# Where three pieces of ScalarE, VectorE and TensorE work stand in the attention projections of a hybrid attention and mLSTM kernel

## The chip, the core and the metric

The kernel runs on one core of one Trainium2 chip. The metric is the device time of one execution in microseconds. Three runs of the kernel before took 1403.57, 1403.64 and 1404.39 us; the median is 1403.64 us.

## What is computed

The model is two layers deep on 512 tokens of width 1024: a dilated window attention, a gated FFN, an mLSTM mixer and a second gated FFN, each with its norm and residual. The change touches only the projections of the attention, and the work that is woven into them:

```python
proj = (xn @ w_in).reshape(B, S, N_GROUPS, 3, ATTN_HEADS, ATTN_HEAD_DIM)   # 3 groups, q k v, 8 heads of 128
for g, (window, dilation) in enumerate(((128, 1), (512, 4), (2048, 16))):
    q = apply_partial_rope(proj[:, :, g, 0], positions) * scale            # only the first 32 of 128 rows turn
    k = apply_partial_rope(proj[:, :, g, 1], positions)
    o, lse = dilated_window_attention(q, k, proj[:, :, g, 2], window, dilation)
wts = softmax(stack(lses), axis=0)                                          # over the three groups
out = (sum over g of wts[g] * o[g]).reshape(B, S, 1024) @ w_out
```

## The kernel before

Every float32 product is made of three matmuls: each operand is split into a rounded part ("hi", written by a cast on ScalarE, L224) and the rest ("lo", a subtraction on VectorE, L226), and hi·hi, lo·hi and hi·lo are added in PSUM. In the trace ACT is ScalarE, DVE VectorE, PE TensorE, SP and POOL the engines that issue DMAs.

The eight heads go in four pairs, a0 to a3. From pair 1 on, group 0 of a pair is projected plainly, and groups 1 and 2 (names a1g1, a1g2 and so on) as a "unit" each, `qk_unit`: the two 1024x256 weight blocks (q and k) and the tokens are cut in halves, and seven products of a Strassen kind give what eight would. Their order is P1, P5, P6, P2, P7, P3, P4; each is 24 matmuls of 128x128 by 128x256. They share three PSUM banks: P1 and P2 add up in `c`, P5 and P3 in `p`, P6, P7 and P4 in `u`. Behind each product stands `finish`: after P1 ScalarE copies bank c to bank u (L903); after P5 and P6 it copies banks p and u to SBUF (`vu`, L906 and L908); after P2 and P4 ScalarE packs the 32 rows to be rotated (`rot`, L897) and copies the bank to the q tile (L916); after P7 and P3 VectorE adds the bank to `vu` into the k tile (L923), and ScalarE packs again. The bank p that P5 of unit g2 fills is the one that the L916 copy behind P4 of unit g1 empties, so the first matmul of P5 waits for that copy (the row `a1g2p <- a1g_q` of the PE waits).

The weights of a unit come in four pieces W11, W12, W21, W22 by SP's DMA queue (L863) into a ring of raw buffers (`a1g2W` and so on); a piece's load is issued when the buffer's last reader is done, which is mostly an L226. `prepare_part` forms differences of pieces on VectorE (`less`, L871) and then the split (L224, L226). `Feed` prepares the splits ahead of their product: `pop` hands over one and fills up to `ahead` (3 here).

Work of other kinds is put into this stream by a clock of ticks (`defer(n, fn)` runs fn n ticks on, `advance` is a tick; a unit ticks after its products 2, 4, 6 and 7). Two kinds matter. First, `rope` turns the packed rows on VectorE (L605 to L614) and returns `back`, which copies them back into q and k on ScalarE: L620 for group 0 (four instructions for q, four for k), L622 for the others. Second, the attention of the pair before, whose places are the table `RUN_AT` (scores of groups 1 and 2, the joint softmax, L792/L795 weights, L801 transposes to and from DRAM, and `values`, L819/L824) and the scores of group 0 of the current pair, `scores0` (matmuls L698, VectorE's mask and maximum L704, exponentials L741 on ScalarE), placed by `SCORES0_AT`. What shares an engine goes in written order, helped by `behind`, which issues work behind the instruction last written on a named engine.

Of the kernel before, what the change touches and what calls it, by code (L numbers as in the profile page):

```python
# [32 lines left out]
C1 = 6.28125  # L33
C2 = float(np.float32(np.uint32(np.float32(TWO_PI - C1).view(np.uint32) & 0xFFFFF000).view(np.float32)))
C3 = float(np.float32(TWO_PI - C1 - C2))
SCORES0_AT = (None, 6, 6, 5)
RUN_AT = (1, (4, 5, 8, 8, 9), (11, 12), (2, 3, 1))
RUN3_AT = (1, (4, 5, 7, 7, 8), (11, 12), (2, 3, 1))
LAST_AT = (1, (2,), (), (1, 1, 1))
STACK_AT = (9, 11, 15, 17)  # L40
HEAD_AT = ((9, 10, 12), (10, 11, 13), (12, 13, 15), (13, 14, 16), (15, 16, 18), (16, 17, 19), (18, 19, 21),
# [33 lines left out]
def tile_hybrid_dilated_attn_mlstm(  # L75
# [205 lines left out]
    class Feed:  # L281
# [6 lines left out]

        def pop(self, _=0):
            whl = self.ready.pop(0) if self.ready else self.plan.pop(0)()  # L290
            while self.plan and len(self.ready) < self.ahead:
                self.ready.append(self.plan.pop(0)())
            return whl

    ends = {}

# [105 lines left out]
    with ExitStack() as actx:  # L402
# [485 lines left out]
        def qk_unit(pr, g, qk):  # L888
            nm = "a%dg%d" % (pr, g)
            last = pr == HEADS // 2 - 1 and g == 2  # L890
            target = {"P1": "c11", "P2": "c11", "P5": "p5", "P3": "p5", "P6": "u", "P7": "u", "P4": "u"}
            two_m = lambda t: t.rearrange("p (m s) -> p m s", m=2)
            acc = {}
            rot = vu = None

            def pack(q, src):
                nc.scalar.activation(two_m(rot[0][quarter(q)]), src, AF.Copy)  # L897

            def finish(name):
                nonlocal rot, vu  # L900
                if name == "P1":
                    acc["u"] = acc_tile(nm + "u")
                    nc.scalar.activation(acc["u"], acc["c11"], AF.Copy)  # L903
                elif name == "P5":
                    vu = ap.tile([P, 2, SEQ], F32, tag="vu", name=nm + "vu")
                    nc.scalar.activation(vu[:, 0], acc["p5"], AF.Copy)  # L906
                elif name == "P6":
                    nc.scalar.activation(vu[:, 1], acc["u"], AF.Copy)  # L908
                elif name in ("P2", "P4"):
                    th = int(name == "P4")  # L910
                    src = two_m(acc[target[name]])
                    if th == 0:
                        t = ap.tile([P, 2, SEQ], F32, tag="rot", name="rot")
                        rot = t[:, 0], t[:, 1]
                    pack(th, src[:R])
                    nc.scalar.activation(halves(qk[0], th), src, AF.Copy)  # L916
                    if last and th:
                        rope(qk, rot, False, 1, 2, True)
                else:
                    th = int(name == "P7")  # L920
                    out = halves(qk[1], th)
                    with behind_scores():
                        nc.vector.tensor_tensor(out, two_m(acc[target[name]]), two_m(vu[:, 1 - th]), op=ALU.add)  # L923
                    pack(2 + th, out[:R])
                    if last and th == 0:
                        rope(qk, rot, False, 0, 1, True)
                        rope(qk, rot, False, 2, 4, True)

            for n, name in enumerate(QK_ORDER):
                key = target[name]  # L930
                if name in ("P1", "P5"):
                    acc[key] = acc_tile(nm + key)
                whl = feed.pop()
                with fenced():
                    for m in range(2):
                        for k in range(4):
                            for a, b in SPLITS:
                                if name in ("P1", "P2", "P4"):
                                    x_ = pair[b][k + 4 * (name != "P1")][:, HALF * (name == "P4"):HALF * (1 + (name == "P4"))]
                                else:  # L940
                                    x_ = sum_part(name, b, k)
                                nc.tensor.matmul(acc[key][:, m * HALF:(m + 1) * HALF], whl[a][:, k, m * P:(m + 1) * P], x_,
                                                 start=(name in ("P1", "P5") and m == 0 and k == 0 and (a, b) == SPLITS[0]),
                                                 stop=(m == 1 and k == 3 and (a, b) == SPLITS[-1]), skip_group_check=True)
                finish(name)
                if n == 6 and not last:
                    back = rope(qk, rot, False)
                    if g == 2:
                        back()
                    else:  # L950
                        defer(1, back)
                if n in (1, 3, 5, 6):
                    advance()

        def project_pair(pr, qks, then=None):
            nm = "a%d" % pr
            for g in range(3):
                base = g * 3 * D + pr * 256
                qk = []
                qks.append(qk)  # L960

                box = []
                if pr and g:
                    qk.extend(tok_tile("%sg%d_%s" % (nm, g, "qk"[part])) for part in range(2))
                    qk_unit(pr, g, qk)
                    continue

                def rot(box=box):
                    if not box:
                        if pr:  # L970
                            box.extend(npl.tile([P, SEQ], F32, tag=tag, name="rot") for tag in ("rbc", "ssum"))
                        else:
                            t = ap.tile([P, 2, SEQ], F32, tag="rot", name="rot")
                            box.extend((t[:, 0], t[:, 1]))
                    return box
                for part in range(2):
                    t = tok_tile("%sg%d_%s" % (nm, g, "qk"[part]))

                    def evac(m, acc, t=t, rot=rot, g=g, part=part):
                        to = rot()  # L980
                        views = (in_order, by_block) if g == 0 else (lambda x: x,) * 2
                        if pr == 0:
                            nc.vector.tensor_tensor(views[0](t[:, m]), views[1](acc), views[1](rbc), op=ALU.mult)
                        else:
                            nc.vector.tensor_copy(views[0](t[:, m]), views[1](acc))
                        for th in range(2):
                            q = 2 * part + th
                            nc.scalar.activation(packed(to, q, m, g == 0), turned((t, t), q, m, g == 0), AF.Copy)
                    if pr == 0 and g == 0 and part == 0:
                        def first_evac(evac=evac):  # L990
                            bc_hook()
                            for m in range(2):
                                evac(m, facc[m])
                        defer(1, first_evac)
                    else:
                        if pr == 0 and g == 2 and part == 1:
                            defer(1, lambda: renew(range(4)))
                        project(pair, w_in, base + part * D, KC, evac, "%sg%d%s" % (nm, g, "qk"[part]), ready=feed,
                                amid=pr > 0 and part == 1)
                    qk.append(t)  # L1000
                    if part == 1:
                        turn = lambda qk=qk, rot=rot, g=g: rope(qk, rot(), g == 0)
                        if pr == 0 and g == 2:
                            postponed.append(lambda: turn()())
                        else:
                            defer(3 if pr else 1, turn())
                    if pr == 0 and 1 <= g:
                        step = 2 * (g - 1) + part
                        (lambda: sum_of("S3"), lambda: sum_of("S4"), lambda: None, lambda: None)[step]()
                        for key in ((), ("W12", "W22"), (), ())[step]:  # L1010
                            for hf in range(2):
                                behind(load_block, 0, key, hf, engine=mybir.EngineType.SP)
                if g == 0 and then is not None:
                    then()
                if g == 0 and pr == 0:
                    first_values()
# [231 lines left out]
        for pr in range(1, HEADS // 2):  # L1248
            qks = []
            following = attention_pair(pr, qks)  # L1250
            follow(todo, RUN3_AT if pr == 3 else RUN_AT)
            project_pair(pr, qks, lambda fn=following[0], pr=pr: defer(SCORES0_AT[pr], lambda: run(fn)))
            todo = following
        last_values, last_bring = todo[3], todo[6]
        run(lambda: todo[1]((1,)))
# [1111 lines left out]
```

## Time and profile before

| | us |
|---|---|
| median of three runs | 1403.64 |
| the profiled execution, its own time | 1403.1 |
| its span in the trace | 1401.2 |
| PE busy | 1373.2 (98 %) |
| DVE busy | 1110.8 (79 %) |
| ACT busy | 798.4 (57 %) |

The granted TensorE clock is 0.997 on the mean. The projections of the pairs 1 to 3 lie between about 200 and 430 us of the span. Rows of the timeline give the start, the duration, engine, line and operation, the output and input, and in square brackets the idle time of the engine just before, with what ended it. In the list of waits a row names the engine and what it wanted to do, what it waited for, then the total, the number of times and the longest, in us. In a table of windows the columns are the busy time of PE, PE's weight loads, DVE, ACT and POOL, the granted clock (PEclk, 1.00 is full), the busy share of the DMA engines and GB/s.

### The profile page before, as it was taken

Reading aid. Unit: us, or ns where it says so; the run is one execution under the profiler, and the core shown is the slowest. Engines: PE = TensorE matmul, PEld = TensorE weight load, DVE = VectorE, ACT = ScalarE, POOL = GpSimd, SP = SyncE. Lnnn points to the kernel's source line nnn. Section 1 sums busy time; section 2 is a strip of 40 time slices with the busy share of each in tenths; the row PEclk is TensorE's granted clock in tenths of the full one; section 3 lists DMA queues with packets and bytes.
Section 4 is the critical chain, followed back from the end, with each engine's and each line's share of the span. In section 5 each row is a group of like instructions: output and inputs, shape, how many; then the busy total and the mean of one; then the engine's idle time right before and its main releaser. Section 6 shows DMA issues by size and latency. Waiting matters only on the chain. (4 is left out here: it accounts for less than half of the span.)

```text
span 1401.2 us, 22635 instructions
## 1 busy us (share of the span) xinstructions
PE 1373.2 (98%) x8740; PEld 1245.5 (89%) x8740; DVE 1110.8 (79%) x1853; ACT 798.4 (57%) x1334; POOL 163.3 (12%) x240
## 2 busy tenths in 40 slices
PE   9999999999979999999999999999999999999997
PEld 7888889889878888999999998888888899999886
DVE  7758669596877289877877898898858987888887
ACT  6556566666655155444566464786534544458854
POOL 3000011111011001000000100113201240001213
PEclk9999999999999999999999999999999999999999
DMA  8534246547375447333253643334334563335963
GB/s 286 183 120 136 89 138 194 160 121 233 89 235 155 150 133 164 121 121 108 90 169 87 144 143 88 93 79 106 95 117 117 136 191 121 121 108 132 196 164 99
DMA packets 140068, 193.82 MB, mean 138 GB/s; under 512 B 8980, under 2 KB 104788, under 8 KB 139960
## 3 DMA queue, kind: packets, MB, share of 16 engines
q1 hardware_dynamic: 119552, 139.81, 31.8%
q0 software_dynamic: 18752, 51.43, 16.0%
q8 instruction: 69, 1.13, 0.3%
q10 hardware_dynamic: 1656, 1.12, 0.2%
q14 instruction: 39, 0.32, 0.1%
HBM read 167.30 MB, written 22.54 MB: 135 GB/s over the span
## 5 line engine op out<-in xcount | busy, mean ns | idle before, releaser
L1670 POOL DMA_DIRECT2D f1T<-in_ffn_w_out_dram x15 | 17.8, 1185 | 209.0 <-DMA f1P_2w_w<-in_ffn_w_out_dram 136.2
L1645 POOL DMA_DIRECT2D f0S<-in_ffn_w_out_dram x10 | 8.7, 874 | 261.0 <-DVE f0hid L1562 173.0
L2202 POOL DMA_DIRECT2D hD<-hB x32 | 21.7, 698 | 68.3 <-DVE hB L2199 68.3
L256 PE MATMUL mo<-n_h,mo_k_l 128*128 128x512 f32 x64 | 25.3, 395 | 0.0
L256 PE MATMUL mo<-n_h,mo_k_h 128*128 128x512 f32 x64 | 25.2, 394 | 0.0
L256 PE MATMUL mo<-n_l,mo_k_h 128*128 128x512 f32 x64 | 25.2, 393 | 0.0
L256 PE MATMUL awo<-ao_h,awo_k_h 128*128 128x512 f32 x64 | 25.2, 393 | 0.0
L256 PE MATMUL mwo<-yo_l,mwo_k_h 128*128 128x512 f32 x64 | 25.1, 392 | 0.0
L256 PE MATMUL mqk<-n_h,mqk_k_h 128*128 128x512 f32 x64 | 25.1, 392 | 0.0
L256 PE MATMUL mqk<-n_l,mqk_k_h 128*128 128x512 f32 x64 | 25.1, 392 | 0.0
L256 PE MATMUL awo<-ao_l,awo_k_h 128*128 128x512 f32 x64 | 25.1, 392 | 0.0
L256 PE MATMUL f0j<-n_h,f0j_h 128*128 128x512 f32 x64 | 25.0, 391 | 0.0
L256 PE MATMUL f1j<-n_h,f1j_h 128*128 128x512 f32 x64 | 25.0, 391 | 0.0
L256 PE MATMUL mwo<-yo_h,mwo_k_l 128*128 128x512 f32 x64 | 25.0, 391 | 0.0
L256 PE MATMUL mqk<-n_h,mqk_k_l 128*128 128x512 f32 x64 | 25.0, 391 | 0.0
L256 PE MATMUL awo<-ao_h,awo_k_l 128*128 128x512 f32 x64 | 25.0, 390 | 0.0
L256 PE MATMUL f1j<-n_h,f1j_l 128*128 128x512 f32 x64 | 24.9, 390 | 0.0
L256 PE MATMUL f0j<-n_h,f0j_l 128*128 128x512 f32 x64 | 24.9, 390 | 0.0
L256 PE MATMUL f0j<-n_l,f0j_h 128*128 128x512 f32 x64 | 24.9, 389 | 0.0
L256 PE MATMUL f1j<-n_l,f1j_h 128*128 128x512 f32 x64 | 24.9, 389 | 0.0
L256 PE MATMUL mwo<-yo_h,mwo_k_h 128*128 128x512 f32 x64 | 24.8, 391 | 0.0
L226 DVE TENSOR_TENSOR v1P_l<-v1W,v1P_h 128x1024 fp32r<-128x1024 f32 x14 | 17.1, 1223 | 9.3 <-ACT v1P_h L224 9.3
(2617 smaller groups left out, 5890.0 us busy)
## 6 DMA issues: line engine op xcount, KB each, us to landing
f0j_w<-in_ffn_w_in_dram SPq DMA_DIRECT2D x17, 512.0 KB, 5.0
f1j_w<-in_ffn_w_in_dram SPq DMA_DIRECT2D x17, 512.0 KB, 6.0
f1T<-in_ffn_w_out_dram POOLq DMA_DIRECT2D x15, 512.0 KB, 7.1
f0hid<-in_ffn_w_in_dram SPq DMA_DIRECT2D x9, 512.0 KB, 6.1
f1hid<-in_ffn_w_in_dram SPq DMA_DIRECT2D x9, 512.0 KB, 5.0
v0W<-in_attn_w_in_dram SPq DMA_DIRECT2D x8, 512.0 KB, 6.4
v1W<-in_attn_w_in_dram SPq DMA_DIRECT2D x8, 512.0 KB, 4.4
awo_k_w<-in_attn_w_out_dram SPq DMA_DIRECT2D x8, 512.0 KB, 4.7
```

What stands on the lines that cost most here:

```text
L226: nc.vector.tensor_tensor(lo[:, :n], raw[:, :n], hi[:, :n].bitcast(F32), op=ALU.subtract)
L256: nc.tensor.matmul(acc, whl[a][:, k, m * P:(m + 1) * P], pairs[b][kk], start=(kk == 0 and (a, b) == SPLITS[0]), stop=(kk == nk - 1 and (a, ...
L1645: nc.gpsimd.dma_start(t, src[1][:, ks], accum_op=ALU.add)
L1670: nc.gpsimd.dma_start(view(to), weight_rows(hk * UNITS + u, n), accum_op=ALU.add)
L2202: nc.gpsimd.dma_start(hD[k // 4].rearrange("(b i) x -> i b x", i=R)[:, :, c0:c0 + R], t[R * a_:R * (a_ + 1)])
```

## The change

Three edits, all in the stream of the pairs 1 to 3.

- The scores of group 0 of pair 3 are asked for 6 ticks on instead of 5, as those of the pairs 1 and 2, and pair 3's table of places for the attention of pair 2 (`RUN3_AT`) is replaced by that of the others.
- `qk_unit` calls `feed.fill(ahead + 1)` right behind `finish`, so the next split is written there, ahead of the deferred work of the tick, and no longer at the next `pop`.
- The `back` of a rope is written behind the instruction that is last on ScalarE at that time (`behind(..., engine=ACT)`).

```diff
-SCORES0_AT = (None, 6, 6, 5)
+SCORES0_AT = 6
 RUN_AT = (1, (4, 5, 8, 8, 9), (11, 12), (2, 3, 1))
-RUN3_AT = (1, (4, 5, 7, 7, 8), (11, 12), (2, 3, 1))
...
         def pop(self, _=0):
             whl = self.ready.pop(0) if self.ready else self.plan.pop(0)()
-            while self.plan and len(self.ready) < self.ahead:
+            self.fill(self.ahead)
+            return whl
+
+        def fill(self, n):
+            while self.plan and len(self.ready) < n:
                 self.ready.append(self.plan.pop(0)())
-            return whl
...
                 finish(name)
+                feed.fill(feed.ahead + 1)
                 if n == 6 and not last:
                     back = rope(qk, rot, False)
                     if g == 2:
                         back()
                     else:
-                        defer(1, back)
+                        defer(1, lambda: behind(back, engine=ACT))
...
-                            defer(3 if pr else 1, turn())
+                            back = turn()
+                            defer(3 if pr else 1, lambda back=back: behind(back, engine=ACT))
...
-            follow(todo, RUN3_AT if pr == 3 else RUN_AT)
-            project_pair(pr, qks, lambda fn=following[0], pr=pr: defer(SCORES0_AT[pr], lambda: run(fn)))
+            follow(todo, RUN_AT)
+            project_pair(pr, qks, lambda fn=following[0]: defer(SCORES0_AT, lambda: run(fn)))
```

Lines after the change have other numbers: L224 and L226 become L223 and L225, L620 L622, L801 L803, L871 L873, L897 L899, L906 and L908 become L908 and L910, L916 L918, L698 L700, L704 L706.

The first place is ScalarE in unit g1 of pair 1. Before, the back of group 0 stands around the copies of P5 and P6 of that unit (L906, L908):

```order
L224 ACTIVATE a1g1P_h<-a1g1W_1585 128x1024
L906 ACTIVATE a1g1vu<-a1g1p_1847 128x512
L620 ACTIVATE a1g_q<-rot 32x4x64 x4
L224 ACTIVATE a1g1P_h<-a1g1W_1587 128x1024
L908 ACTIVATE a1g1vu<-a1g1u 128x512
L620 ACTIVATE a1g_k<-rot 32x4x64 x4
```

After, the same eight copies (now L622) stand at the end of the unit, behind the last cast, which is that of P6 of unit g2, and ahead of the packing (L899) and the bank copy (L918) of P4 of unit g1:

```order
L899 ACTIVATE rot<-a1g_k 32x512 x2
L223 ACTIVATE a1g2P_h<-a1g2W_1853 128x1024
L622 ACTIVATE a1g_q<-rot 32x4x64 x4
L622 ACTIVATE a1g_k<-rot 32x4x64 x4
L899 ACTIVATE rot<-a1g1u 32x512
L918 ACTIVATE a1g_q<-a1g1u 128x2x256
```

The pairs 2 and 3 have the same pattern. The second place is VectorE at the same time of pair 1. Before, the transposes of pair 0 (L801) stand ahead of the lo of P3 (from W_1585) and of P4:

```order
L614 TENSOR_TENSOR rot<-rot 128x512
L226 TENSOR_TENSOR a1g1P_l<-a1g1W_1583,a1g1P_h 128x1024
L801 STREAM_TRANSPOSE a0pB<-a0p_1529 128x15x4x32
L226 TENSOR_TENSOR a1g1P_l<-a1g1W_1585,a1g1P_h 128x1024
L226 TENSOR_TENSOR a1g1P_l<-a1g1W_1587,a1g1P_h 128x1024
```

After, the lo of P3 stands ahead of the transposes:

```order
L616 TENSOR_TENSOR rot<-rot 128x512
L225 TENSOR_TENSOR a1g1P_l<-a1g1W_1583,a1g1P_h 128x1024
L225 TENSOR_TENSOR a1g1P_l<-a1g1W_1585,a1g1P_h 128x1024
L803 STREAM_TRANSPOSE a0pB<-a0p_1529 128x15x4x32
L225 TENSOR_TENSOR a1g1P_l<-a1g1W_1587,a1g1P_h 128x1024
```

The third place is unit g2 of pair 3, the last of the phase. On VectorE before, the lo of P3 (from W_3525) stands behind the rotation of q's first rows (L605, L606) and all sixteen rows of the scores' mask and maximum (L704):

```order
L226 TENSOR_TENSOR a3g2P_l<-a3g2W_3486,a3g2P_h 128x1024
L605 STREAM_SHUFFLE rot<-rot 32x512
L606 TENSOR_TENSOR rot<-rot,cosn 32x512
L704 ISA a3p_3778,a3own<-a3s_3780,acst 128x128
...
L704 ISA a3p_3779,a3own<-a3s_3795,acst 128x256
L704 ISA a3own 128x1
L736 TENSOR_SCALAR a3nb<-a3own 128x4
L226 TENSOR_TENSOR a3g2P_l<-a3g2W_3525,a3g2P_h 128x1024
```

After, the lo of P3 (from W_3518), the lo of P4 and the lo of the first value weights (`a3g12v`) stand ahead of them:

```order
L225 TENSOR_TENSOR a3g2P_l<-a3g2W_3485,a3g2P_h 128x1024
L616 TENSOR_TENSOR rot<-rot 128x512
L873 TENSOR_TENSOR a3g2W_3556<-a3g2W_3556,a3g2W_3483 128x1024
L225 TENSOR_TENSOR a3g2P_l<-a3g2W_3518,a3g2P_h 128x1024
L225 TENSOR_TENSOR a3g2P_l<-a3g2W_3556,a3g2P_h 128x1024
L225 TENSOR_TENSOR a3g12v_k_l<-a3g12v_k_w,a3g12v_k_h 128x1024
L607 STREAM_SHUFFLE rot<-rot 32x512
L608 TENSOR_TENSOR rot<-rot,cosn 32x512
L609 TENSOR_TENSOR rot<-rot,sinn 32x512
L613 TENSOR_TENSOR a3g_q<-rot 32x2x256
L706 ISA a3p_3845,a3own<-a3s_3847,acst 128x128
```

On TensorE the matmuls of `scores0` of pair 3 stood between P5 and P6 of unit g2; after, they stand between P2 and P7, as in the pairs 1 and 2. Nothing else on TensorE changes place.

## The prediction

> **What bounds the kernel now.** I read the shares first, then the waits of the engine with the largest share, then the timeline around the waits that the change can touch.
>
> ```profile
> span 1401.2 us, 22635 instructions
> PE 1373.2 (98%) x8740; PEld 1245.5 (89%) x8740; DVE 1110.8 (79%) x1853; ACT 798.4 (57%) x1334; POOL 163.3 (12%) x240
> ```
>
> TensorE is busy for 98 % of the span, and the change adds or removes no matmul. It can only move time between TensorE's waits. So the question is which waits of TensorE the three edits remove and which they make. The list of its waits, longest first, with the rows of the pairs 1 to 3:
>
> ```profile
> PE a3g2p L942 <- DVE a3g2P_l L226: 5.5, 1, 5.5
> PE a3g2p L942 <- ACT a3g_q L916: 2.0, 1, 2.0
> PE a3o L819 <- DMA a3pT<-a3pD: 1.6, 1, 1.6
> ...
> PE a2g1u L942 <- ACT a2g1vu L908: 1.1, 1, 1.1
> PE a1g2p L942 <- ACT a1g_q L916: 1.0, 1, 1.0
> ...
> PE a2g2p L942 <- ACT a2g_q L916: 0.7, 1, 0.7
> ```
>
> Two kinds matter. One is a single stall of 5.5 us, P3 of unit g2 of pair 3 waiting for its lo. The other is the wait at the seam of the two units of each pair: P5 of g2 needs bank p, and ScalarE's L916 copy behind P4 of g1 is late by 1.0, 0.7 and 2.0 us. The change removes the first and puts 2.9 us of ScalarE work ahead of the second.
>
> **The change part by part.** The seam of pair 1 first, on ScalarE and VectorE:
>
> ```profile
> 214.43 1.46 ACT L620 ACTIVATE a1g_q<-rot 32x256 f32<-32x256 f32 x4 [1.50 <-DVE rot L614]
> 217.49 1.45 ACT L620 ACTIVATE a1g_k<-rot 32x256 f32<-32x256 f32 x4
> ...
> 224.95 0.68 DVE L923 TENSOR_TENSOR a1g_k<-a1g1p,a1g1vu 128x512 f32<-128x512 f32 x1
> 226.60 1.23 DVE L871 TENSOR_TENSOR a1g2W<-a1g2W,a1g2W 128x1024 f32<-128x1024 f32 x1 [0.97 <-DMA a1g2W<-in_attn_w_in_dram]
> ...
> 227.94 1.06 ACT L224 ACTIVATE a1g2P_h<-a1g2W 128x1024 fp32r<-128x1024 f32 x1 [1.65 <-DVE a1g2W L871]
> 229.03 0.59 ACT L897 ACTIVATE rot<-a1g1u 32x512 f32<-32x512 f32 x1
> 229.64 0.60 ACT L916 ACTIVATE a1g_q<-a1g1u 128x512 f32<-128x512 f32 x1
> ...
> 230.29 0.50 PE L942 MATMUL a1g2p<-S,a1g2P_h 128*128 128x256 f32 x2 [1.01 <-ACT a1g_q L916]
> ```
>
> ScalarE has no gap between the cast of P6 of g2 (227.94) and the end of the bank copy (230.24): 2.30 us for cast, pack and copy. In the new order the two backs, 1.46 + 1.45 = 2.91 us, stand between cast and pack. So from the start of that cast the copy now ends 2.30 + 2.91 = 5.21 us later. If nothing else moved, P5 would start 2.91 us late in each pair. But the cast itself waits (1.65 us) for a difference on VectorE, which waits for a DMA (0.97 us): piece W22 of g2's weights. That load is issued when a buffer comes free, which is the end of the lo of g1's P3, here behind the transposes:
>
> ```profile
> 215.46 2.17 DVE L801 STREAM_TRANSPOSE a0pB<-a0p 128x1920 f32<-128x1920 f32 x1
> 217.55 2.31 DVE L226 TENSOR_TENSOR a1g1P_l<-a1g1W,a1g1P_h 128x1024 fp32r<-128x1024 f32 x2
> ...
> 218.76 1.50 SPq L863 DMA_DIRECT2D a1g2W<-in_attn_w_in_dram  x2
> ```
>
> Now that lo stands ahead of the transposes. It can start at 215.5, since its cast is done at 212.4, so the load is issued about 2.1 us earlier and should land near 224.5 instead of 226.6. Then the difference is bound by VectorE itself: its k addition (224.95) waits for P3 on TensorE, which comes 0.35 us earlier, because ScalarE's copy of P6 (L908) no longer stands behind the back and TensorE's wait for it (0.4 us) goes. So the difference starts near 225.3 in place of 226.60, the cast 1.3 us earlier at 226.6, and the copy ends at 226.6 + 5.21 = 231.8 against 230.24. **Pair 1: +1.6 us.** Its bounds: +1.3 (all of the 1.65 us idle time goes) to +2.9 (the load lands no earlier).
>
> The same in pair 2:
>
> ```profile
> 299.84 1.23 DVE L226 TENSOR_TENSOR a2g2P_l<-a2g2W,a2g2P_h 128x1024 fp32r<-128x1024 f32 x1 [0.32 <-ACT a2g2P_h L224]
> ...
> 306.09 1.23 DVE L871 TENSOR_TENSOR a2g2W<-a2g2W,a2g2W 128x1024 f32<-128x1024 f32 x1 [0.42 <-DMA a2g2W<-in_attn_w_in_dram]
> ...
> 307.43 1.07 ACT L224 ACTIVATE a2g2P_h<-a2g2W 128x1024 fp32r<-128x1024 f32 x1 [1.10 <-DVE a2g2W L871]
> ```
>
> Less can be won back here: the DMA wait is 0.42 us, and a VectorE wait for a cast of 0.32 us goes because that cast no longer stands behind a back. Cast at 307.43 − 0.74 = 306.7, copy done 5.21 later at 311.9, against P5's start at 309.78. **Pair 2: +2.2 us** (bounds +1.8, all 1.10 us back, to +2.9).
>
> In pair 3 the seam was already worse, and for another reason:
>
> ```profile
> 384.08 1.13 DVE L795 TENSOR_SCALAR a2p<-a2p,a2cf 128x256 f32<-128x256 f32 x4
> 385.13 1.22 DVE L871 TENSOR_TENSOR a3g2W<-a3g2W,a3g2W 128x1024 f32<-128x1024 f32 x1
> ...
> 386.29 2.00 ACT L224 ACTIVATE a3g2P_h<-a3g2W 128x1024 fp32r<-128x1024 f32 x2 [1.46 <-DMA a3g2W<-in_attn_w_in_dram]
> 388.93 0.60 ACT L916 ACTIVATE a3g_q<-a3g1u 128x512 f32<-128x512 f32 x1
> 389.58 0.50 PE L942 MATMUL a3g2p<-S,a3g2P_h 128*128 128x256 f32 x2 [1.96 <-ACT a3g_q L916]
> ```
>
> Pair 3's own table puts four weight multiplications (1.13 us) ahead of the difference, and two casts stand ahead of the copy. With the common table the difference comes first, at about 383.8, and one cast of the two goes behind the copy: cast 385.05, copy done at 390.26. **Seam of pair 3: +0.7 us** (bounds −0.3, when the cast starts a microsecond earlier still, to +2.0, the 2.9 less the one cast).
>
> Then the large stall. VectorE's queue in unit g2 of pair 3:
>
> ```profile
> 403.36 1.06 ACT L224 ACTIVATE a3g12v_k_h<-a3g12v_k_w 128x1024 fp32r<-128x1024 f32 x1 [3.28 <-DMA a3g12v_k_w<-in_attn_w_in_dram]
> ...
> 404.94 0.01 DVE L605 LOAD_MASK_SELECT rot<-rot  x1 [8.42 <-ACT rot L897]
> ...
> 406.29 0.27 DVE L704 CUSTOM_DVE_ANT_0 a3p<-a3s,acst 128x128 f32<-128x128 f32 x1
> ...
> 408.85 1.21 DVE L226 TENSOR_TENSOR a3g2P_l<-a3g2W,a3g2P_h 128x1024 fp32r<-128x1024 f32 x1
> ...
> 410.11 0.58 PE L942 MATMUL a3g2p<-S4h,a3g2P_l 128*128 128x256 f32 x1 [5.50 <-DVE a3g2P_l L226]
> ...
> 414.08 1.72 PE L819 MATMUL a2o<-a2pT,a2v 128*128 128x128 f32 x14
> ```
>
> The chain reads backwards: P3's lo stands behind the score maxima, these behind the rotation of q's rows, that behind ScalarE's pack, that behind the cast of the value weights, and that behind their DMA, which lands at 403.3. VectorE idles for 8.42 us with a lo in its queue that needed none of this. In the new order the lo of P3 stands ahead of the rotation, so it is done before TensorE comes to P3, and the wait of 5.50 us goes. With it goes a slow stretch behind it:
>
> ```profile
> 406.00:410.00 4.00, 0.00 (x0) 0.00 (x0) 4.00 (x20) 1.04 (x5) 0.00 (x0) 0.94 0.52 198
> 411.00:412.00 1.00, 1.00 (x7) 1.00 (x7) 1.00 (x2) 1.00 (x5) 0.00 (x0) 0.50 0.48 131
> 413.00:414.00 1.00, 1.00 (x11) 1.00 (x10) 0.90 (x2) 0.82 (x2) 0.00 (x0) 1.00 0.76 178
> 388.00:390.00 2.00, 0.42 (x3) 0.42 (x4) 2.00 (x4) 1.95 (x4) 1.27 (x3) 1.00 0.19 40
> ```
>
> TensorE went idle at 404.6; the clock fell to half at about 409.5, and 13 matmuls came 0.21 instead of 0.12 us apart (x7 against x11 in a microsecond): 1.2 us more. The 1.96 us wait at the seam left the clock full.
>
> What is late next? P3 would end at about 407.9 (it began at 404.3; 0.7 for the seam; 24 x 0.12 = 2.9), and behind it stand the values of pair 2 (414.08 before). They need the PSUM bank that the sixth of the eight score maxima frees, and these still stand behind the value weights: their load is issued about 1 us earlier (its buffer is freed by an earlier lo), so it lands near 401.7 to 402.3; cast 1.06, lo 1.21, shuffle, two products and an addition some 2.5, six maxima 1.8: 408.3 to 408.9. With the hand-over I take the values' start at 409.1, a new wait of 1.25 us (bounds 0 to 3). It starts 414.08 − 409.1 = 5.0 us earlier than before, the seam's 0.7 included. **Pair 3: −5.0 us.** Behind this the order is as before, and the wait for a3pT hangs on the last scores and moves along.
>
> The edits that only shift a split ahead of a tick's work elsewhere change nothing that TensorE waits for in that list; I take them at 0.
>
> **Sum:** 1.6 + 2.2 − 5.0 = −1.2 us on the profiled run, whose own time is 1403.1: 1401.9. The median of the runs is 0.5 us above it: 1402.4. Bounds without a new slow clock: best 1.3 + 1.8 − 7.2 (no wait for the maxima, seam of pair 3 at −0.3) = −4.1; worst 2.9 + 2.9 − 2.0 (seam +2.0 and a wait of 3) = +3.8.
>
> The new waits at the seams would be 1.0 + 0.4 + 1.6 = 3.0 us, 0.7 + 1.1 + 0.6 + 2.2 less what TensorE wins ahead of it = 3.5, and 2.0 + 0.7 + 0.6 = 3.3. The longest that left the clock full is 1.96, the one that halved it 5.5. [...]
>
> **The rivals.**
>
> *Slower: the seams cost in full and the clock falls.* If W22 lands no earlier, because the earlier load shares the DMA engines with the pieces issued just ahead of it, the copy is late by 2.9 us in pairs 1 and 2 and by 2.0 in pair 3; the waits become 3.9 to 4.6 us, and each may halve the clock, at 1.2 us each. It decides at a landing later than about 225.3 in pair 1. Price: 2.9 + 2.9 + 2.0 − 5.7 + 3.6 = +5.7, about 1409; with one halving of three, +3.3, 1407. For it: the idle time at the seams was short already, and the cover is worth at most 1.65 us. Against it: the load is issued 2 us earlier by the order of the rows. Chance 0.17.
>
> *The clock falls without that.* A gap of 3.0 to 3.5 us lies between the two that the trace shows. If all three trip, −1.2 + 3.6 = +2.4: 1406. [...] Chance 0.10.
>
> *Faster.* The value weights land as early as 401 and VectorE is through before P3 ends, and the differences come as early as ScalarE can take them: −3 to −4, about 1400. For it: the bank rule asks only for the sixth maximum. Against it: it needs every bound at its good end. Chance 0.20.
>
> *The stall stays in another form.* If the value weights land as late as before, at 403.3, the values of pair 2 wait until 410.2: pair 3 gives only −3.9, and the sum is −0.1, 1403.5. Chance 0.13.
>
> The forecast has the remaining 0.40.
>
> **How the numbers follow.** A measurement of this kernel tells about 0.2 % (2.8 us) from no change. The forecast and the last rival lie within it, as does the fallen clock for the most part; of the faster rival some three quarters, and some of the forecast's lower half, lie beyond. Faster 0.22, within 0.2 % 0.59, slower 0.19. The range reaches down to the faster rival, 1399.3, and up to one tripped clock with seams in full, 1407.
>
> **What would show it.** In the waits of TensorE after: no row of P3 on its lo in pair 3; the seam rows (a1g2p, a2g2p, a3g2p waiting for the L918 copy) at 3.0, 3.5 and 3.3 us; the rows for `vu` in g1 gone; a new row of a2o waiting for pair 3's maxima near 1.25 us; a granted clock of 1.00 at all these places. Wrong would be: seam rows above 4 us, a PEclk of 0.5 behind them, or a2o waiting for 3 us. If the back does not delay the bank copy at all, my reading of ScalarE's queue has failed.

## The result, and the profile after

The changed kernel took 1402.84 us (median of 12 runs, 1400.59 to 1407.38); the kernel before, in 12 runs beside it, 1403.54 us (1400.07 to 1406.10). The ratio is 0.9996, with a 95 % interval of 0.9985 to 1.0008: no difference that this measurement can tell. The forecast was 1402.4. The profiled execution took 1400.59 us with a span of 1398.8 us.

The total stands still, and yet almost every wait in the list of TensorE's has changed. The waits of TensorE after, longest first (engine, what it wanted, what it waited for, total, times, longest):

```profile
PE a2g2p L944 <- ACT a2g_q L918: 2.8, 1, 2.8
PE a3g2p L944 <- ACT a3g_q L918: 2.8, 1, 2.8
PE a1g2p L944 <- ACT a1g_q L918: 2.8, 1, 2.8
...
PE a3o L821 <- DMA a3pT<-a3pD: 1.1, 1, 1.1
PE a3s L724 <- DVE a3g_q L613: 1.0, 1, 1.0
...
PE a1o L821 <- DVE a2own L706: 0.7, 1, 0.7
```

The 5.5 us wait of P3 is gone, and so are the rows of group g1 that waited for `vu` and for the k addition. In their place stand three seams of 2.8 us, the same to 0.1 us in each pair (forecast: 3.0, 3.5 and 3.3), and two rows that were not there before: the values of pair 1 wait for pair 2's score maxima, and the last scores of pair 3 wait for q's rotated rows. The seam of pair 1 in the timeline, on ScalarE and then TensorE:

```profile
226.81 1.06 ACT L223 ACTIVATE a1g2P_h<-a1g2W 128x1024 fp32r<-128x1024 f32 x1 [0.58 <-DVE a1g2W L873]
227.77 1.45 ACT L622 ACTIVATE a1g_q<-rot 32x256 f32<-32x256 f32 x4
229.23 1.45 ACT L622 ACTIVATE a1g_k<-rot 32x256 f32<-32x256 f32 x4
230.71 0.59 ACT L899 ACTIVATE rot<-a1g1u 32x512 f32<-32x512 f32 x1
231.32 0.60 ACT L918 ACTIVATE a1g_q<-a1g1u 128x512 f32<-128x512 f32 x1
...
231.97 0.50 PE L944 MATMUL a1g2p<-S,a1g2P_h 128*128 128x256 f32 x2 [2.77 <-ACT a1g_q L918]
```

The difference that the cast waits for no longer waits for its DMA; the cast starts 1.13 us earlier than before (226.81 against 227.94). Then the 2.9 us of copies follow without a gap, and the bank copy ends at 231.92.

What came behind the seams is in the windows (PEclk, the granted clock, is the third number from the end). The three stretches of 1 us behind the seams of pairs 1, 2 and 3:

```profile
233.00:234.00 1.00, 1.00 (x7) 1.00 (x6) 1.00 (x2) 1.00 (x3) 1.00 (x3) 0.50 0.86 177
313.00:314.00 1.00, 1.00 (x11) 1.00 (x10) 0.75 (x2) 1.00 (x3) 1.00 (x3) 1.00 0.37 81
394.00:395.00 1.00, 1.00 (x7) 1.00 (x7) 1.00 (x3) 0.63 (x1) 1.00 (x3) 0.50 0.82 159
```

After two of three equal waits the clock was halved, from 232.69 to 236.10 and from 393.11 to 396.52 us, 3.41 us each time; each stretch cost 1.5 us. Last, unit g2 of pair 3, where the stall stood:

```profile
398.42 1.22 DVE L225 TENSOR_TENSOR a3g2P_l<-a3g2W,a3g2P_h 128x1024 fp32r<-128x1024 f32 x1
402.33 1.23 DVE L225 TENSOR_TENSOR a3g2P_l<-a3g2W,a3g2P_h 128x1024 fp32r<-128x1024 f32 x1 [2.69 <-ACT a3g2P_h L223]
405.53 1.23 DVE L225 TENSOR_TENSOR a3g12v_k_l<-a3g12v_k_w,a3g12v_k_h 128x1024 fp32r<-128x1024 f32 x1 [1.97 <-ACT a3g12v_k_h L223]
...
409.45 0.27 DVE L706 CUSTOM_DVE_ANT_0 a3p<-a3s,acst 128x128 f32<-128x128 f32 x1
...
411.37 0.82 PE L821 MATMUL a2o<-a2pT,a2v 128*128 128x128 f32 x5
...
427.20 1.60 PE L724 MATMUL a3s<-a3g_k,a3g_q 128*128 128x128 f32 x12 [0.99 <-DVE a3g_q L613]
```

P3's lo is done at 399.6, 8.7 us before TensorE comes to P3 (408.26). The maxima still stand behind the value weights.

Where the time went is told best by TensorE's own positions: for each group of matmuls, the start in the trace after minus the start in the trace before. Plus is later.

| group | shift, us | what lies between it and the row above |
|---|---|---|
| P1 of a1g2 | −0.08 | the wait for P6's copy gone |
| P5 of a1g2 | +1.68 | seam of pair 1: +1.76 |
| P6 of a1g2 | +3.18 | half clock: +1.50 |
| P1 of a2g2 | +0.39 | −2.79: 0.6 in the pair's scores, 2.2 in waits of a2g1 that are gone |
| P5 of a2g2 | +2.53 | seam of pair 2: +2.14, clock full |
| values of pair 1 | +3.36 | their wait for the maxima |
| P1 of a3g2 | +1.72 | −1.75: waits of a3g1 that are gone |
| P5 of a3g2 | +2.56 | seam of pair 3: +0.84 |
| P3 of a3g2 | +4.05 | half clock: +1.5 (the moved scores lie in between in both) |
| values of pair 2 | −2.71 | the stall gone: −6.76 |
| value projection, after the last scores | −1.36 | the new wait for q, and what it brings: +1.25 |
| output projection (awo) | −1.25 | |

The waits of g1 that are gone are these rows of the kernel before, beside the 1.1 us of pair 2 for `vu`; they make 1.7 of the 2.2 us and 1.2 of the 1.75 us, and the rest stands in no row of the list:

```profile
PE a2g1u L942 <- DVE a2g_k L923: 0.6, 1, 0.6
PE a3g1u L942 <- ACT a3g1vu L908: 0.6, 1, 0.6
PE a3g1u L942 <- DVE a3g_k L923: 0.6, 1, 0.6
```

In this pair of traces the attention phase ends 1.25 us earlier. The other 1.2 us between the two spans arise behind it, where the order of the instructions is the same, and are less than the runs of one kernel differ among themselves.

### The profile page after: what moved, and what is told of

Its sections match the earlier page's. It is cut to its first block, busy times and chain, and to the rows that moved or that the text cites. A ratio compares the mean times of both kernels' runs of the same rounds, so it can differ in the third digit from the quotient of the medians.

```text
span 1398.8 us, 22646 instructions
## 1 busy us (share of the span) xinstructions
PE 1374.3 (98%) x8740; PEld 1247.2 (89%) x8740; DVE 1110.6 (79%) x1853; ACT 799.1 (57%) x1334; POOL 163.8 (12%) x240
## 3 DMA queue, kind: packets, MB, share of 16 engines
q8 instruction: 69, 1.13, 0.3%
## 5 line engine op out<-in xcount | busy, mean ns | idle before, releaser
L225 DVE TENSOR_TENSOR v1P_l<-v1W,v1P_h 128x1024 fp32r<-128x1024 f32 x14 | 17.1, 1224 | 9.3 <-ACT v1P_h L223 9.3
```

What stands on the lines that cost most here:

```text
L225: nc.vector.tensor_tensor(lo[:, :n], raw[:, :n], hi[:, :n].bitcast(F32), op=ALU.subtract)
```

## The experiments

Theory after the result: three separate mechanisms, each of them in one edit. The table removes the stall. The place of group 0's back makes the seams. The early split makes the waits for maxima. The rivals are named with each run. Times are medians, save in two kernels of a single run; "before" is the kernel before on the same chip, and the ratio is to it. Of the third edit only group 0's back was moved by itself; the back of a unit's last rows, which is also written later, was not. Neither were the two lines of the table's edit tried apart. In the edits three points stand for lines of the change that are left out.

**The changed kernel once more**, in a second profiled execution, to see whether the clock falls behind the same seams.

> The changed kernel once more, for one look at the same three seams. [...] Rival: the half clock belongs to the place; then it follows the seams of pairs 1 and 3 again and not that of pair 2.

1402.34 us in this single run. Its windows at the same three places:

```profile
233.00:234.00 1.00, 1.00 (x6) 1.00 (x6) 1.00 (x2) 1.00 (x2) 1.00 (x3) 0.50 0.87 182
313.00:314.00 1.00, 1.00 (x11) 1.00 (x10) 0.79 (x1) 1.00 (x3) 1.00 (x3) 1.00 0.43 92
395.00:396.00 1.00, 1.00 (x11) 1.00 (x10) 1.00 (x2) 1.00 (x2) 1.00 (x3) 1.00 0.85 179
```

The seams waited 2.7, 2.8 and 2.8 us again; the clock fell at pair 1 only. So the half clock of pair 3 is not a property of the place. Pair 1's clock fell both times. The waits for maxima varied as well: 2.5 us at the values of pair 1 (0.7 in the first execution) and 1.9 at those of pair 2 (less than 0.3 in the first). In this execution the output projection starts 0.42 us later than in the trace before, not 1.25 us earlier.

**The table alone.**

```diff
-SCORES0_AT = (None, 6, 6, 5)
+SCORES0_AT = 6
...
-            follow(todo, RUN3_AT if pr == 3 else RUN_AT)
+            follow(todo, RUN_AT)
...
```

> The kernel before with only the first edit: pair 3 gets the places of the other pairs (scores of group 0 at 6 ticks, the common table), no early split, rotated rows copied back where they were. My theory: the 5.5 us wait of P3 in pair 3 goes by this edit alone, since it moves the score maxima behind P3's lo; the seam waits of pairs 1 and 2 stay at 1.0 and 0.7 us, the waits for the copies of P6 (0.4, 1.1, 0.6) stay, no halved clock at the seams. About 5 us less than before, some 1398.5. Rival: the early split is what puts the lo ahead; then the wait stays above 4 us and the time stays within 1.5 us of before.

1400.38 us against 1403.34, ratio 0.9981 (0.9972 to 0.9991), 2 us above the expected 1398.5. The stall is gone by this edit alone, and TensorE is 8.6 us ahead at the values of pair 2. But only 3.1 us are left at the output projection. The waits of this kernel and a row of its ScalarE show where they went:

```profile
PE a3s L721 <- DVE a3g_q L610: 3.3, 1, 3.3
...
PE a3s L721 <- ACT o_keep L633: 1.6, 1, 1.6
...
PE a3g1u L941 <- ACT a3g1vu L907: 1.1, 1, 1.1
PE a2g1u L941 <- ACT a2g1vu L907: 1.0, 1, 1.0
```

```profile
409.50 1.06 ACT L223 ACTIVATE a3g12v_k_h<-a3g12v_k_w 128x1024 fp32r<-128x1024 f32 x1 [8.07 <-DMA a3g12v_k_w<-in_attn_w_in_dram]
```

The last scores need rotated rows. Their packing stands on ScalarE behind the exponentials, and these behind the cast of the second piece of value weights, for which ScalarE waits 8.07 us. So in this kernel the end of pair 3 hangs on a load, and TensorE cannot profit from arriving earlier by more than that load allows.

**The early split alone.**

```diff
...
                 finish(name)
+                feed.fill(feed.ahead + 1)
```

> The kernel before with the early split alone: pair 3's own table and the rotated rows as before. My theory: the 5.5 us wait of P3 goes by this edit too, since the lo of P3 is written ahead of the tick's scores; but the values of pair 0 wait some 4.5 us for pair 1's maxima, as they did without the late rotated rows. So about no gain against before, 1402 to 1404. Rival: the wait in pair 1 came from the moved copy of the last unit's rows; then there is none here, and the time is 1397 to 1399.

1407.92 us against 1402.11, ratio 1.0037 (1.0026 to 1.0047): slower, which neither theory gave. The stall of P3 is gone here too, but the waits for maxima are 5.8, 1.1 and 2.7 us. VectorE and ScalarE of this kernel in pair 1, with the first row of the wait list:

```profile
PE a0o L822 <- DVE a1own L707: 5.8, 1, 5.8
```

```profile
249.35 1.23 DVE L226 TENSOR_TENSOR a2g0q_k_l<-a2g0q_k_w,a2g0q_k_h 128x1024 fp32r<-128x1024 f32 x1 [6.92 <-ACT a2g0q_k_h L224]
250.49 0.28 DVE L707 CUSTOM_DVE_ANT_0 a1p<-a1s,acst 128x128 f32<-128x128 f32 x1
```

```profile
248.26 1.06 ACT L224 ACTIVATE a2g0q_k_h<-a2g0q_k_w 128x1024 fp32r<-128x1024 f32 x1 [6.14 <-DMA a2g0q_k_w<-in_attn_w_in_dram]
```

The next pair's first split stands ahead of pair 1's maxima. ScalarE waits 6.14 us for its weights, VectorE 6.92 us for ScalarE, and the values of pair 0 wait for a bank that the maxima free. The clock was at half behind it (the mean granted clock of the profiled run is 0.995, that of the kernel before 0.997). At the values of pair 1 TensorE was 6.0 us later than before, which the removed stall no longer made up.

**Group 0's back where it was.** All else as changed.

```diff
-                            defer(3 if pr else 1, lambda back=back: behind(back, engine=ACT))
+                            defer(3 if pr else 1, back)
```

> The changed kernel, but group 0's rotated rows are copied back where they were (around the copies of P5 and P6). My theory: the seam waits fall from 2.8 us in each pair to 0.5 to 1.5 us, the waits for the copies of P6 come back (0.4 to 1.1), no halved clock at any seam, and the time is 4 to 6 us below before, some 1398. Rival: the seams are late by the early split or by the weights' load; then they stay above 2 us with the clock halved at some, and the time stays at the changed kernel's 1403.

1404.29 us against 1403.34, ratio 1.0007 (0.9997 to 1.0016). The seams fell as expected (0.4 us at pair 2, none above 0.2 elsewhere), but the time did not: the values of pair 0 wait 4.5 us for the maxima, with the clock at half behind (mean granted clock of the profiled run 0.995). Pair 2's values wait 2.0 us more:

```profile
PE a0o L821 <- DVE a1own L706: 4.5, 1, 4.5
PE a2o L821 <- DVE a3own L706: 2.0, 1, 2.0
```

The expectation of 1398 missed because it left out the early split. Pair 1's maxima begin at nearly the same time in both kernels (248.95 us in the changed one, 249.32 here), but there TensorE comes to the values of pair 0 only at 250.95. So in the changed kernel the seam of pair 1 makes TensorE late and hides that wait; take the seam away and the wait is there.

**Without the early split.**

```diff
                 finish(name)
-                feed.fill(feed.ahead + 1)
```

> The changed kernel without the early split (no fill behind finish). The rotated rows now stand ahead of the last cast instead of behind it, still ahead of the bank copy. My theory now: the early split puts the next pair's first split ahead of the score maxima, so that these wait for its load, which is the wait of the values of the pair before (0.7 to 4.5 us so far); without it those waits go in the pairs 1 and 2, while the seams still wait 2 to 2.8 us with the clock halved at some. Time 1400 to 1402, between the table alone and the changed kernel. Rival: the maxima wait for the rotated rows, not for the load; then the values' waits stay at 0.7 us and more.

1401.29 us against 1402.11, ratio 0.9996 (0.9987 to 1.0005). No values wait for maxima any more; the seams wait 2.3, 2.6 and 2.6 us:

```profile
PE a3s L724 <- DVE a3g_q L613: 2.8, 1, 2.8
PE a3g2p L944 <- ACT a3g_q L918: 2.6, 1, 2.6
PE a2g2p L944 <- ACT a2g_q L918: 2.6, 1, 2.6
PE a1g2p L944 <- ACT a1g_q L918: 2.3, 1, 2.3
```

So the waits for maxima belong to the early split, and the seams to the back. All traces together settle the rival. In the seven with the early split, pair 1's first maximum starts 2.2 to 2.5 us behind the landing of the next pair's first weights, whenever they land (243.8 to 248.2 us); in the six without it, it starts 1.1 to 4.5 us ahead of that landing. TensorE was 5.7 us ahead at the values of pair 2 and gave back 4.7 at the last scores.

**Group 0's back twice**, in the same place; the second copy writes the same values, so it only adds time.

```diff
-                            defer(3 if pr else 1, lambda back=back: behind(back, engine=ACT))
+                            defer(3 if pr else 1, lambda back=back: (behind(back, engine=ACT), pr and behind(back, engine=ACT)))
```

> The changed kernel with group 0's rotated rows copied back twice in the same place (the second copy writes the same values). My theory: each seam waits 2.9 us more, 5.7 us in place of 2.8, and now the clock falls at all three seams; about 9 us of waits more, and at most 3 us of slow clock more. Rival: ScalarE's copies are not what the bank copy waits for; then the seams stay within 1 us of 2.8.

1409.55 us in a single run. Waits and windows:

```profile
PE a2g2p L944 <- ACT a2g_q L918: 5.8, 1, 5.8
PE a3g2p L944 <- ACT a3g_q L918: 5.8, 1, 5.8
PE a1g2p L944 <- ACT a1g_q L918: 5.8, 1, 5.8
```

```profile
235.00:236.00 1.00, 1.00 (x7) 1.00 (x7) 1.00 (x3) 1.00 (x3) 0.00 (x0) 0.50 1.00 284
318.00:319.00 1.00, 1.00 (x6) 1.00 (x6) 1.00 (x3) 1.00 (x2) 0.00 (x0) 0.50 0.89 236
402.00:403.00 1.00, 1.00 (x6) 1.00 (x7) 1.00 (x2) 1.00 (x2) 0.00 (x0) 0.50 0.86 207
```

5.8 − 2.8 = 3.0 us more for 2.9 us of copies: ScalarE's copies are the seam, one for one. All three seams now halve the clock.

**Group 0's back two ticks later**, behind the bank copy.

```diff
-                            defer(3 if pr else 1, lambda back=back: behind(back, engine=ACT))
+                            defer(5 if pr else 1, lambda back=back: behind(back, engine=ACT))
```

> The changed kernel, but group 0's rotated rows go back two ticks later: behind the bank copy of P4, behind the copies of banks c and p in unit 2, ahead of the copy of its P6. My theory: neither the seam nor the copies of P6 wait for them: seams at 0.3 to 1.0 us, no waits for P6's copy, clock full; 6 to 8 us below before, some 1396.5, the fastest. Rival: the rows come too late for group 0's scores behind P2, and TensorE waits there by 1 to 3 us in each pair; then the time is 1400 to 1404.

1401.86 us against 1403.34, ratio 0.9995 (0.9986 to 1.0004). The rival held, with a longer wait in pair 1 than it named: the seam is gone and the scores of group 0 wait instead.

```profile
PE a1s L700 <- ACT a1g_k L622: 4.5, 1, 4.5
PE a3s L700 <- ACT a3g_k L622: 2.4, 1, 2.4
PE a2s L700 <- ACT a2g_k L622: 2.4, 1, 2.4
```

**Group 0's back one tick earlier, with the table, without the early split.** It now stands behind P2's bank copy, where ScalarE idled. The table's lines are those of the run of the table alone.

```diff
...
-                            defer(3 if pr else 1, turn())
+                            back = turn()
+                            defer(2 if pr else 1, lambda back=back: behind(back, engine=ACT))
```

> The table alone, and group 0's rotated rows copied back 2 ticks on instead of 3, behind P2's bank copy, where ScalarE idled for 3 us; no early split. My theory: the waits for P6's copy go in every pair (0.4, 1.0, 1.1), the seams stay below 0.8 us, no values wait for maxima; the time is 1 to 3 us below the table alone, some 1398, though part is given back at the end of pair 3, where the last scores wait for rows that hang on the value weights' load. Rival: the end of pair 3 takes it all; then the time is that of the table alone, 1400.4, with a wait of the last scores above 5 us.

1396.33 us against 1402.11, ratio 0.9959 (0.9945 to 0.9972): faster than before, which the changed kernel is not. Some of its waits:

```profile
PE a3g2p L941 <- ACT a3g_q L915: 2.4, 1, 2.4
...
PE a2g1u L941 <- DVE a2g_k L922: 1.3, 1, 1.3
...
PE a3g1u L941 <- DVE a3g_k L922: 1.0, 1, 1.0
...
PE a3s L721 <- DVE a3g_q L610: 0.4, 1, 0.4
```

The waits of g1 for P6's copies are gone, but those for the k addition behind them rise from 0.6 us to 1.3 and 1.0. The seams are 1.0, 0.4 and 2.4 us. At the last, two casts stand ahead of the copy and wait for a load, as in the kernel before; it halved the clock (P5's matmuls came 0.21 us apart until 390.9 and 0.12 us apart from then on) and missed the expected 0.8.

**The same three placings on one chip.** First all three edits with the back at 2 ticks, then the run above again, then the table alone again. The edit of the first:

```diff
-                            defer(3 if pr else 1, lambda back=back: behind(back, engine=ACT))
+                            defer(2 if pr else 1, lambda back=back: behind(back, engine=ACT))
```

> The changed kernel with all three edits, only group 0's rotated rows 2 ticks on instead of 3, behind P2's bank copy. Against the next two runs it has the early split and the late copy of the last unit's rows besides. My theory: the seams are short as without the early split, but the values of pair 0 wait 3 to 6 us for pair 1's maxima with the clock halved behind, since the next pair's first split stands ahead of these; 1401 to 1404, 5 us above the same placing without the early split. Rival: the early split costs only where the rotated rows are late; then the time is within 1.5 us of 1396.3.

> The table with the rotated rows 2 ticks on, without the early split, once more, beside the table alone on the same chip. My theory: 1396 to 1397 again, 3 to 4 us below the table alone, of which 1.2 us in the trace are the waits for P6's copies of pairs 2 and 3, and the rest the last scores' wait for q at the end of pair 3, which depends on when the value weights land. Rival: the earlier distance was the chip's; then the two lie within 1.5 us.

> The table alone once more, beside the two others on the same chip. My theory: 1400 to 1401 again, with a wait of the last scores of 3 us or more for q's rows at the end of pair 3. Rival: that wait is chance of one execution; then it is below 1 us here and the time near 1398.

| on one chip, before 1402.93 us | us | ratio (95 %) | TensorE's shift at awo, us |
|---|---|---|---|
| table, back at 2 ticks, early split | 1398.72 | 0.9964 (0.9951 to 0.9978) | −2.7 |
| table, back at 2 ticks | 1396.24 | 0.9949 (0.9937 to 0.9961) | −6.0 |
| table alone | 1400.43 | 0.9982 (0.9973 to 0.9992) | −1.7 |

With the back at 2 ticks, the early split and the later copy of the unit's last rows cost 2.5 us together: half of what I expected. This time the values of pair 0 waited only 0.8 us for pair 1's maxima, since the next pair's weights landed at 243.8 us and not at 247.1 as with group 0's back where it was; those of pair 1 waited 3.6 us, with the clock at half behind (0.50). Moving the back gains 4.2 us over the table alone. None of that gain is there yet at the values of pair 2: TensorE reaches them 1.8 us later than with the table alone (1.3 us in the first traces of the two). It all arises at the last scores. In the trace of the table alone the last scores again wait 3.2 us for q, so that was no chance; with the back at 2 ticks they wait 0.4 us or nothing. In those two traces the heads' load (oT) is issued ahead of the value weights and all six value loads follow in one go; with the table alone it stands between the first two and the other four, and the slowest value load takes 10.3 to 10.5 us to land in place of 8.1 to 8.7. Whether the order of these loads makes that difference was not tried.

## Why the prediction was right

The time and the range were right. The sign is not shown, since the measured difference of −0.7 us is within the noise. The sum for the attention phase (−1.2 us) is what the first trace shows (−1.25), and that agreement is luck: the second shows +0.42, and in the first several terms that I left at nothing nearly cancel. What stands ahead of the seams returned 4.5 us, the halved clock took 3.0, pair 2's maxima 0.8 and the last scores 1.25, together some +0.5; the stall gave 1.1 us more than forecast.

- **The seams.** Forecast +1.6, +2.2 and +0.7 us; measured +1.76, +2.14 and +0.84. The working (cast, then 2.9 us of copies, then pack and bank copy, less what the difference gains by the earlier load) holds in pair 1, row by row, and the doubled back shows the price one for one.
- **What stands ahead of a seam.** I counted 0.35 and 0.74 us for waits that go in g1 of pairs 1 and 2, and only as cover for the seam. In fact the waits that go in the pairs 2 and 3 returned 2.2 and 1.75 us of TensorE time that pair 1 had lost. This is the step "Less can be won back here": each pair was worked out against the old positions, as if the pair before had cost nothing. By its sum TensorE would have been 3.8 and 4.5 us late at P5 of g2 in the pairs 2 and 3; it was 2.5 and 2.6, though a halved clock had cost 1.5 in between.
- **The clock.** I took the clock as full behind the new waits of 3.0 to 3.5 us, a term of 0 us in the sum that no run shows: gaps of 2.7 to 2.8 us halved it in three seams of six, 1.5 us each, 3.0 us in the profiled execution. A PEclk of 0.5 behind the seams is one of the signs of being wrong that the prediction named. The second rival had the halved clock, at a somewhat small price (1.2 us each) and with too small a chance (0.10, for all three).
- **The stall.** Forecast −5.7 us net of the seam, with a new wait of 1.25 us for the maxima. It went whole, with the slow stretch behind it: net of seam and clock it gave −6.76, and no wait for the maxima of 0.3 us or more came. That, too, is luck. I had the value weights issued 1 us earlier and landing at 401.7 to 402.3 us; they were issued at 397.21 (396.96 before) and landed at 404.33 (403.26 before), so the sixth maximum was done only at about 411.3. TensorE, late by the seam and the clock, came to the values at 411.37. So the condition of the last rival, weights as late as before, held without its price. In the second execution the values had to wait 1.9 us.
- **Behind the stall.** "Behind this the order is as before" was the second failed step: the last scores wait for rows that stand on ScalarE behind the exponentials, and through them hang on the value weights' load. It cost 1.25 us here, and 4.7 to 6.6 us with the table alone (both traces) and without the early split, where TensorE arrives 5.7 to 8.6 us earlier. With the back at 2 ticks and no early split TensorE arrives 6.4 and 7.4 us earlier, and it cost only 0.4 and 0.9. So this end is the largest reason why the table alone gave 2.5 to 3 us and not 6.7; what sets it, beyond the order of the loads that goes with it, stays open.
- **The early split**, which I took at 0 where it only shifts a split: it is not free. It was hidden in pair 1 of the changed kernel by the very delay that the back makes, and made the kernel 5.8 us slower as the only edit, with the stall gone.

So the changed kernel holds one useful edit, the table (−0.18 to −0.19 %), and two that eat it. With the table, the back one tick earlier than in the kernel before ran 0.41 to 0.51 % below before; that it does is shown, why it does is not.

## What to carry to other kernels

In these traces a queue passed on the wait of what stood ahead in it (with the early split alone, 6.1 us of waiting for weights on ScalarE became 6.9 on VectorE and 5.8 on TensorE); so before moving an instruction up, ask what it waits for, above all a load, and who stands behind it. When several waits are in a row, work out the shift of each stretch from the one before and not from the old trace, and follow it to the end of the phase, where a load may fix the end whatever the engine gained. A delay can hide another wait, so undo edits one at a time and also try each alone.

## What the runs showed of the hardware

In these traces the length of a wait of TensorE did not decide alone whether its clock was halved behind it. Waits of 1.6 us and more between 196 and 480 us of the span, in us, by the granted clock behind them, as far as it was read:

| wait | clock behind it 1.00 | clock behind it 0.50 |
|---|---|---|
| 1.6 to 1.96 | kernel before (1.6, 1.96), table alone (1.63, 1.79) | none |
| 2.1 to 3.3 | changed kernel (2.80), once more (2.8, 2.8), table alone (3.26), all three edits with the back at 2 ticks (2.14) | changed kernel (2.77, 2.79), once more (2.7), table alone again (3.24), table with the back at 2 ticks (2.43, again 2.22) |
| 3.6 and more | none | kernel before (5.50), all three edits with the back at 2 ticks (3.64), group 0's back where it was (4.5), group 0's back twice (5.8, 5.8, 5.8), early split alone (5.8) |

For three of these the clock is read from the distance of the matmuls: 0.23 us between those of 128x512 behind 1.63 and 1.79 us, and 0.21 us between those of 128x256 behind 2.43 us. In the traces of the kernel before and of the changed kernel, each of the three stretches at half clock in this part of the span lasted 3.41 us.

The seam of pair 3 came out either way in the two executions of the changed kernel. So did the last scores of pair 3 in the two profiles of the table alone, after 3.26 and 3.24 us of waiting. The first:

```profile
425.00:426.00 1.00, 0.66 (x5) 0.66 (x6) 0.97 (x8) 0.00 (x0) 0.00 (x0) 1.00 0.14 29
426.00:427.00 1.00, 1.00 (x10) 0.98 (x9) 1.00 (x11) 0.00 (x0) 0.00 (x0) 1.00 0.63 76
427.00:428.00 1.00, 1.00 (x6) 0.81 (x5) 1.00 (x12) 0.00 (x0) 0.00 (x0) 1.00 0.83 299
```

The second:

```profile
425.00:426.00 1.00, 0.72 (x4) 0.73 (x5) 0.97 (x8) 0.00 (x0) 0.00 (x0) 0.70 0.11 25
426.00:427.00 1.00, 1.00 (x6) 1.00 (x6) 1.00 (x11) 0.00 (x0) 0.00 (x0) 0.50 0.45 92
427.00:428.00 1.00, 1.00 (x7) 1.00 (x6) 0.45 (x6) 0.00 (x0) 0.00 (x0) 0.50 0.81 309
```

What besides the length decides between the two was not shown.
